# A hybrid encoder trunk on one core: buffers, engines and instruction order at the end of the recurrent scan and at the start of two output projections

## The chip, the core and the metric

The kernel runs on one core of a Trainium2 chip. Its engines work side by side, each through its own list of instructions in a fixed order: TensorE (PE in the profile) multiplies matrices, VectorE (DVE), ScalarE (ACT) and GpSimd (POOL) work on tiles, and SyncE (SP) issues most transfers between device memory and SBUF. An instruction waits until its operands are there and its output tile is free, and whatever stands behind it on the same engine waits with it. The metric is the device time of one execution in microseconds, the median of several runs.

## The reference

Two batches (256 prompt tokens, 1024 sample tokens, 1024 channels) go through two layers. Layer 0 mixes tokens with a bidirectional recurrence, layer 1 with neighbourhood attention. Each ends in an output projection, a residual sum and a squared-ReLU MLP. What matters here:

```
y = sum over both directions of _wkv_scan(...)            # per head, 64 wide
mu = mean(y); var = mean((y - mu)^2)                      # per token and head
y = (y - mu) * rsqrt(var + GN_EPS) * lnx_g + lnx_b
y = y + bonus * v
g = sigmoid(xg @ g1) @ g2                                 # the gate, 160 inner channels
x = x + (y * g) @ w_o                                     # layer 0
x = x + sq_relu_mlp(rms_norm(x, g_mlp), w_up, w_down)
...
x = x + attention(...) @ w_no                             # layer 1 (na_o in the reference)
x = x + sq_relu_mlp(rms_norm(x, g_mlp), w_up, w_down)
```

## The kernel before

Matrices are multiplied in three passes. An operand is split into a high part (a cast to fp32r, on ACT, tile names with h or hi) and a low part (operand minus high part, names with l or lo), and `mm3` sums high·high, high·low and low·high. Tokens come in three segments `SEGS`: segment 0 is the prompt (256 columns), 1 and 2 are the two halves of the sample (512 each). A tile `x13` is channel block 3 of segment 1. In the trace buffer numbers are left out; `x` stands for all of them.

**Scan.** Ten jobs of 16 steps run one after the other. Work is put in by due times (`at(t, f)`). In each step ACT copies the state `S` (L1101), the vectors `up`, `uv` and the output `y` or `y2` from PSUM, and DVE multiplies `zz` (L1008). After a job, `scan_post` normalises its output in two halves: mean, square, variance, scaling (DVE and ACT), the factor `lnx_g` (L1162) and the sum with the bonus (L1198), four transposes on PE into `zps`, a copy to the tile `zt` (L1207, ACT) and eight stores of `zt` to the scratch array `z_d` (L1212). For the last job (`left == 0`) the stores go through SP, sixteen in all. Before, there is one `zt` buffer.

**Gate.** `gate_begin` puts work into the last job: loads of the gate's operands into `graw`, their seven casts (L1331, L1334), the first two weights of `w_o` with their two casts (L1344), and the subtractions for the low parts on POOL. `gated` then makes 24 units (8 channel blocks times 3 segments): a load of `z_d` into `ot` (L1369, six buffers), four matrix products on PE, one multiply-add on DVE (L1374), a cast on ACT (L1376), a subtraction on DVE or POOL (L1377).

**mixer7**, called once for `w_o` and once for `w_no`. Its first stretch is the loop `for m in range(8)`: for output block m of segment 1, `dense` makes 24 products of 128x512, `take` adds the residual (L1410, DVE) and stores the sum (L1472, SP), `square` adds its square to `ms1` (ACT, POOL). Inside the loop weights are loaded three ahead into four ring slots and cut into high and low part (L1500 on ACT, L1407 on DVE). The weights are used twice. The second use, in the order `order = [0, 4, 1, 5, ...]`, serves segments 0 and 2. Its first three weights (here called order0, order1, order2) are loaded and cut inside the loop, at m = 5, 6 and 7. The fourth, order3, and the scaling of the finished `x1k` tiles (`ahs`, `als`, L1523, L1525; and L1528 in place) belong to the events behind the loop. Weight number n (0 to 7 the first use, 8 onwards the second) lies in ring slot n mod 4, so order0 takes the slot of weight 4 and order3 takes that of weight 7.

The order on an engine is set by a scheduler that moves instructions, except inside a `manual_schedule`, which keeps the engines that it names in the order of the program. Instructions from outside can still be placed among those of such a block. Before, `gated` had none, and the first stretch named SP alone.

Of the kernel before, what the change touches and what calls it, by code (L numbers as in the profile page):

```python
# [5 lines left out]
F32 = mybir.dt.float32  # L6
F32R = mybir.dt.float32r
AF = mybir.ActivationFunctionType
ALU = mybir.AluOpType
# [4 lines left out]
P = 128  # L14
# [47 lines left out]
class Trunk:  # L62
# [766 lines left out]
    def at(self, t, f):  # L829
        self.todo.append((t, len(self.todo), f))  # L830
# [304 lines left out]
    def scan_post(self, at, J, grp, left):  # L1135

        nc = self.nc
        for half in range(2):
            st = {}
# [12 lines left out]
                bonus = self.bonus.rearrange("p m c -> p (m c)")[:, o0:2 * o1 - o0].rearrange("p (x c) -> p x c", x=2)[:, :, 0:4]  # L1152
                nc.vector.tensor_tensor(out=st["bv"].rearrange("p (x c) v -> p x c v", x=2), in0=view(J["v"]), in1=each(bonus), op=ALU.mult)

            end = nc.gpsimd if left or half == 0 else nc.vector

            def lnx(st=st, runs=runs, y=y, end=end):
                t = y()
# [44 lines left out]
                    nc.tensor.transpose(ps[:, b].rearrange("p e t -> p (e t)"), y()[:, b // 2, b % 2 * 2:b % 2 * 2 + 2].rearrange("p c v -> p (c v)"), self.ident)  # L1203

            def p5(st=st, runs=runs):
                zt = self.yp.tile([P, 4, 2, 64], F32, name="zt", tag="zt", bufs=1)
                nc.scalar.copy(zt, st["zps"])  # L1207
                for x, (m, c0) in enumerate(runs):
                    dst = self.scr["z_d"][m].rearrange("(e v) (c t) -> e v c t", e=2, t=64)
                    for par in range(2):  # L1210
                        for e in range(2):
                            (nc.gpsimd if left else nc.sync).dma_start(dst[e, :, c0 + par:c0 + 4:2], zt[64 * par:64 * par + 64, 2 * x:2 * x + 2, 1 - e])  # L1212
# [87 lines left out]
    def gate_begin(self):  # L1300


        nc, tc = self.nc, self.tc
        at = lambda t, f, *x: self.at(16.0 * (len(self.jobs) - 1) + t, lambda: f(*x))

        def begin():
            self.ectx.close()
            self.m7ctx, self.gctx = ExitStack(), ExitStack()
            pool = lambda c, name, bufs: c.enter_context(tc.tile_pool(name=name, bufs=bufs, reuse_waits="tile", side="right"))
            self.mixer_weights(self.m7ctx, False)  # L1310
            gp = self.gp = pool(self.gctx, "gp", 1)
            self.gate = [[gp.tile([P if i < 2 else 96, n], F32R, name=nm + "hls"[i]) for i in range(3)] for nm, n in (("sg", T), ("g", 1024))]
            gp.tile([P, 512], F32, name="graw", tag="graw", bufs=7)
            self.wo = []

        def load(src, c0, c1, stacked):
            raw = self.gp.tile([P, 512], F32, name="graw", tag="graw", bufs=7)
            raw = raw[:, :c1 - c0]
            if stacked:
                for j in range(3):  # L1320
                    nc.sync.dma_start(raw[32 * j:32 * j + 32], src[P:P + 32, c0:c1])
            else:
                nc.sync.dma_start(raw, src[:P, c0:c1])
            self.graws.append(raw)

        def cut(i, c0, c1, stacked):
            raw = self.graws.pop(0)
            hi, lo, st = (z[:, c0:c1] for z in self.gate[i])
            if stacked:
                low = slice(32, 64) if i else slice(64, 96)  # L1330
                nc.scalar.copy(st, raw[:96])  # L1331
                nc.gpsimd.tensor_tensor(out=st[low], in0=raw[low], in1=st[low].bitcast(F32), op=ALU.subtract)
            else:
                nc.scalar.copy(hi, raw)  # L1334
                nc.gpsimd.tensor_tensor(out=lo, in0=raw, in1=hi.bitcast(F32), op=ALU.subtract)

        def wload(m):
            nc.sync.dma_start(self.m7["raw"][:, m], self.a["w_o"][m])

        def weight(m):  # L1340
            M = self.m7
            raw, (hi, lo) = M["raw"][:, m], M["ring"][m]
            M["turn"][0] += 1
            nc.scalar.copy(hi, raw)  # L1344
            nc.gpsimd.tensor_tensor(out=lo, in0=raw, in1=hi.bitcast(F32), op=ALU.subtract)
            self.wo.append((hi, lo))
        self.graws = []
        at(2.0, begin)
        parts = [(i, c0, min(c0 + 512, n), st) for i, n in ((0, T), (1, 1024)) for st in (0, 1) for c0 in range(0, n, 512)]
        for k, (i, c0, c1, st) in enumerate(parts):  # L1350
            src = self.a["g2"] if i else self.scr["sg2_d"]
            t = 7.0 + 0.9 * k
            at(t - 2.0, load, src, c0, c1, st)
            at(t, cut, i, c0, c1, st)
        for m in range(2):
            at(8.5 + m, wload, m)
            at(11.55 + 1.8 * m, weight, m)

    def gated(self, bank, src):

        nc, act = self.nc, self.act
        with self.gctx, self.tc.tile_pool(name="go", bufs=1, reuse_waits="tile", side="right") as gp:
            (sh, sl, ss), (gh, gl, gs) = self.gate
            todo = [(0, k) for k in range(KT)] + [(s, k) for s in (1, 2) for k in range(KT - 1)] + [(1, KT - 1), (2, KT - 1)]
            for s, k in todo:
                c0, c1 = SEGS[s]
                n = c1 - c0
                t = gp.tile([P, 512], F32, name="ot", tag="ot", bufs=6)[:, :n]
                nc.sync.dma_start(t, self.scr[src][k, :, c0:c1])  # L1369
                ks = slice(k * P, (k + 1) * P)  # L1370
                ps = bank()
                self.mm3(ps[:, :n], gh[:, ks], gl[:, ks], sh[:, c0:c1], sl[:, c0:c1], True, False)
                nc.tensor.matmul(ps[:, :n], gs[:, ks], ss[:, c0:c1], start=False, stop=True)
                nc.vector.scalar_tensor_tensor(out=t, in0=t, scalar=self.v(V_LNB, k), in1=ps[:, :n], op0=ALU.add, op1=ALU.mult)  # L1374
                hi, lo = (z[:, c0:c1] for z in act[k])
                nc.scalar.copy(hi, t)  # L1376
                (nc.gpsimd if k % 2 else nc.vector).tensor_tensor(out=lo, in0=t, in1=hi.bitcast(F32), op=ALU.subtract)  # L1377

    def mixer_weights(self, ctx, both):

# [10 lines left out]
    def mixer7(self, layer, x_src, wname, dst, src=None, gnext=None):  # L1391

        nc, tc, a, act = self.nc, self.tc, self.a, self.act
# [27 lines left out]
        with ExitStack() as ctx:  # L1421
# [70 lines left out]
            order = [0, 4, 1, 5, 2, 6, 3, 7]  # L1492
            todo = [*range(len(wo), 8), *order]

            with tc.manual_schedule(engines={mybir.EngineType.SP}):
                for m in range(8):
                    w = wo.pop(0)
                    while len(wo) < 3:
                        raw, (hi, lo) = wraw(todo.pop(0)), slot()
                        nc.scalar.copy(hi, raw)  # L1500
                        sub(V, lo, raw, hi.bitcast(F32))
                        wo.append((hi, lo))
                    if m == 0:
                        xload(1, 0, 4)
                    elif m < 3:
                        xload(1, 2 * m + 2, 2 * m + 4, m - 1)
                    elif m < 7:
                        xload(2, 2 * m - 6, 2 * m - 4, m - 1)
                    else:
                        xload(0, 0, 8, m - 1)  # L1510
                    take(1, m, dense(w, 1))
                    f = square(1, m)
                    if f:
                        f()
# [49 lines left out]
            for i, m in enumerate(order):  # L1564
                t = MS * i
# [1249 lines left out]
```

## Time and profile before

| what | value |
|---|---|
| median of 3 runs | 3889.02 us (3874.99, 3889.02, 4441.08) |
| profiled execution, its time | 3891.0 us |
| its span | 3889.2 us |
| busy PE, DVE, ACT, POOL | 93%, 71%, 47%, 52% of the span |
| last job's end and gate | about 1290 to 1372 us of the span |
| first stretch with w_o, with w_no | 1369 to 1410 us, 2951 to 2995 us |

The time of the execution is 1.8 us more than its span. Positions below are microseconds from the start of the span. "Idle before" in a row is the time that the engine did nothing ahead of this instruction, and the arrow names what ended it.

### The profile page before, as it was taken

To read this page: it belongs to the slowest core of one execution; us is meant where nothing else is said; L and a number is where in the kernel's file an instruction comes from. 1 tells how busy PE (TensorE), PEld (TensorE's weight loads), DVE (VectorE), ACT (ScalarE), POOL (GpSimd) and SP (SyncE) were. 2 spreads that over 40 slices of the span, in tenths; PEclk is the share of its full clock that TensorE was granted. 3 is DMA by queue.
4 is the path that set the end of the run, shared out by engine and by line. 5 is a ranking of instruction groups with operands and counts; after the bars stand their busy time and mean duration, and the time that the engine had idled before them with its cause. 6 is when DMAs were issued, how large, how long until landed. Compare 5 with 4: busy or idle time off the path is not lost.

```text
span 3889.2 us, 82949 instructions
## 1 busy us (share of the span) xinstructions
PE 3611.9 (93%) x32308; PEld 2979.9 (77%) x32308; DVE 2746.5 (71%) x4265; ACT 1809.9 (47%) x4065; POOL 2017.6 (52%) x2037
## 2 busy tenths in 40 slices
PE   6889998887878799999999999999999999999999
PEld 4766668766766587888888889777777788888888
DVE  7897976477776457777577771466676777767777
ACT  6776763344545445555421132456565455542111
POOL 5451111356566535444588870355454544448887
PEclk8998989889999899999999999999999999999999
DMA  3326666667687453555566635333345255556664
GB/s 110 90 85 212 233 229 186 156 149 176 151 177 169 121 181 120 204 216 212 190 232 234 233 116 162 99 81 74 85 101 185 82 216 212 210 202 219 232 226 162
DMA packets 489847, 654.09 MB, mean 168 GB/s; under 512 B 172752, under 2 KB 347056, under 8 KB 489456
## 3 DMA queue, kind: packets, MB, share of 16 engines
q1 hardware_dynamic: 398416, 436.30, 37.4%
q0 software_dynamic: 44336, 151.15, 11.8%
q10 hardware_dynamic: 46704, 61.35, 4.6%
q8 instruction: 255, 4.18, 0.5%
q14 instruction: 136, 1.11, 0.1%
HBM read 405.47 MB, written 254.41 MB: 170 GB/s over the span
## 4 chain that ended last, share of the span: by engine, by line
PE 44%; DVE 15%; DMA 8%; ACT 6%; issue 5%; POOL 5%; SPq 1%; DVEq 0%; POOLq 0%; ACTq 0%
PE pd L1404 19%; PE ps L1404 8%; DMA h_d<-ho 5%; PE kps L1003 2%; DVE ho L1407 2%; PE ps L108 2%; DVE wlo L1407 2%; POOL tT L1407 1%; PE ps L109 1%; PE ps L110 1%; ACT ho L1705 1%; PE bo L1044 1%; PE ba L1044 1%; PE op L2724 1%; DVE q L894 1%
## 5 line engine op out<-in xcount | busy, mean ns | idle before, releaser
L1404 PE MATMUL pd<-h,whi 128*128 128x512 f32 (+1 forms) x2656 | 697.0, 352 | 0.0
L1410 DVE TENSOR_TENSOR acc<-acc,pd 128x1024 f32<-128x1024 f32 x464 | 559.1, 1207 | 179.8 <-PE pd L1404 146.2
L1404 PEld LDWEIGHTS pd<-h,whi 128*128 128x128 f32 x2656 | 468.2, 189 | 67.9
L1404 PE MATMUL pd<-h,wlo 128*128 128x512 f32 (+1 forms) x1328 | 465.7, 351 | 0.0
L1404 PE MATMUL ps<-ahs,whi 128*128 128x512 f32 x768 | 303.8, 396 | 9.1 <-ACT tq L1748 5.8
L1404 PE MATMUL ps<-als,whi 128*128 128x512 f32 x768 | 300.0, 391 | 2.2 <-DVE als L1525 1.5
L1404 PE MATMUL ps<-ahs,wlo 128*128 128x512 f32 x768 | 299.1, 389 | 0.0
L1404 PEld LDWEIGHTS pd<-h,wlo 128*128 128x128 f32 x1328 | 250.9, 189 | 34.1
L1008 DVE TENSOR_TENSOR zz<-kps,cst 128x512 f32<-128x512 f32 x160 | 110.7, 692 | 179.7 <-ACT ll L1013 179.5
L1864 ACT CAST whi<-rsum 128x512 fp32r<-128x512 f32 x112 | 69.7, 623 | 297.5 <-POOL rsum L1407 162.6
L2638 POOL TENSOR_TENSOR s<-s,mx 128x384 f32<-128x384 f32 (+1 forms) x154 | 119.8, 788 | 156.9 <-DVE mx L2635 146.3
L1864 ACT CAST whi<-raw 128x512 fp32r<-128x512 f32 x128 | 79.3, 620 | 259.9 <-PE pd L1404 256.5
L1003 PE MATMUL kps<-x 64*64 64x128 f32 (+1 forms) x2560 | 169.6, 320 | 23.6 <-issue 17.9
L1407 POOL TENSOR_TENSOR wlo<-raw,whi 128x512 fp32r<-128x512 f32 (+1 forms) x122 | 161.4, 1323 | 56.3 <-ACT whi L1864 55.7
L1404 PE MATMUL ps<-ahp,whi 128*128 128x256 f32 x640 | 179.5, 280 | 0.0
L1404 PE MATMUL ps<-alp,whi 128*128 128x256 f32 x640 | 178.5, 279 | 0.0
L1404 PE MATMUL ps<-ahp,wlo 128*128 128x256 f32 x640 | 178.4, 279 | 0.0
L1404 PEld LDWEIGHTS ps<-ahs,whi 128*128 128x128 f32 x768 | 144.3, 188 | 43.9 <-ACT tq L1748 11.3
L1404 PE MATMUL ps<-op,whi 128*128 128x512 f32 x512 | 165.9, 402 | 11.6 <-DVE op L1407 6.0
L1407 POOL TENSOR_TENSOR wlo<-rsum,whi 128x512 fp32r<-128x512 f32 (+1 forms) x114 | 150.2, 1317 | 42.2 <-ACT whi L1864 38.4
L1404 PEld LDWEIGHTS ps<-als,whi 128*128 128x128 f32 x768 | 144.3, 188 | 33.4 <-DVE als L1525 3.2
L1410 POOL TENSOR_TENSOR rsum<-raw 128x512 f32<-128x512 f32 x60 | 77.4, 1290 | 177.8 <-DMA raw<-in_w_up_dram 165.5
(462 smaller groups left out, 11208.2 us busy)
## 6 DMA issues: line engine op xcount, KB each, us to landing
h<-h_d POOLq DMA_DIRECT2D x116, 1024.0 KB, 8.1
h_d<-ho SPq DMA_DIRECT2D x204, 512.0 KB
x<-x_d SPq DMA_DIRECT2D x80, 512.0 KB
raw<-in_w_up_dram SPq DMA_DIRECT2D x64, 512.0 KB
raw<-in_w_down_dram SPq DMA_DIRECT2D x32, 1024.0 KB
x_d<-ar ACTq DMA_DIRECT2D x32, 512.0 KB
x_d<-bk ACTq DMA_DIRECT2D x32, 512.0 KB
h_d<-ho SPq DMA_DIRECT2D x60, 256.0 KB
```

The lines of the kernel that those rows point to most:

```text
L108: mm(ps, sh, mh, start=first, stop=False)
L109: mm(ps, sh, ml, start=False, stop=False)
L110: mm(ps, sl, mh, start=False, stop=last)
L894: nc.vector.tensor_tensor(out=q[:, 0:jj, jj:], in0=q[:, 0:jj, jj:], in1=tv, op=ALU.add)
L1003: mm(J["kp"][out, e, 192 * c + 192 - w:192 * c + 192], x[es, b, 2 * pr + c], x[es, 5 - w // 64:5, 2 * pr + c], start=True, stop=True)
L1008: nc.vector.tensor_tensor(out=z, in0=src[:, :, :, :P], in1=self.mask[d].unsqueeze(1).unsqueeze(1).to_broadcast([P, 2, 2, P]), op=ALU.mult)
L1044: mm = lambda out, a, b, start, stop: nc.tensor.matmul(out, a, b, start=start, stop=stop, skip_group_check=True)
L1404: mul(ps, w[wi], b[bi], start=first and i == 0, stop=last and i == 2, skip_group_check=True)
L1407: eng.tensor_tensor(out=out, in0=x, in1=y, op=ALU.subtract)
L1410: eng.tensor_tensor(out=out, in0=x, in1=y, op=ALU.add)
L1864: nc.scalar.copy(hi, src)
L2638: nc.gpsimd.tensor_tensor(out=s()[:, :nk], in0=s()[:, :nk], in1=K["mx"][:, 2:3].to_broadcast([P, nk]), op=ALU.mult)
```

## The change

There are five edits. `zt` gets two buffers. The last job's first half does L1162 and L1198 on DVE, as its second half did before. The nine casts of `gate_begin` go from ACT to DVE, with due times a little moved. `gated` keeps program order on PE, DVE, ACT and POOL, and issues each subtraction one unit later. The first stretch of `mixer7` keeps program order on PE, DVE, ACT and POOL as well as on SP.

```
-            end = nc.gpsimd if left or half == 0 else nc.vector
+            end = nc.gpsimd if left else nc.vector
...
-                zt = self.yp.tile([P, 4, 2, 64], F32, name="zt", tag="zt", bufs=1)
+                zt = self.yp.tile([P, 4, 2, 64], F32, name="zt", tag="zt", bufs=2)
...
-                nc.scalar.copy(st, raw[:96])
+                nc.vector.tensor_copy(out=st, in_=raw[:96])
...
-                nc.scalar.copy(hi, raw)
+                nc.vector.tensor_copy(out=hi, in_=raw)
...
-            nc.scalar.copy(hi, raw)
+            nc.vector.tensor_copy(out=hi, in_=raw)
...
-            t = 7.0 + 0.9 * k
+            t = 6.78 + 0.9 * k
...
-            at(11.55 + 1.8 * m, weight, m)
+            at(11.7 + 2.0 * m, weight, m)
...
-        with self.gctx, self.tc.tile_pool(name="go", bufs=1, reuse_waits="tile", side="right") as gp:
+        E = mybir.EngineType
+        back = [lambda: None]
+        with self.gctx, self.tc.tile_pool(name="go", bufs=1, reuse_waits="tile", side="right") as gp, self.tc.manual_schedule(engines={E.PE, E.DVE, E.Activation, E.Pool}):
...
-                (nc.gpsimd if k % 2 else nc.vector).tensor_tensor(out=lo, in0=t, in1=hi.bitcast(F32), op=ALU.subtract)
+                back.append(lambda eng=nc.gpsimd if k % 2 else nc.vector, lo=lo, t=t, hi=hi: eng.tensor_tensor(out=lo, in0=t, in1=hi.bitcast(F32), op=ALU.subtract))
+                back.pop(0)()
+            back.pop(0)()
...
-            with tc.manual_schedule(engines={mybir.EngineType.SP}):
+            with tc.manual_schedule(engines={mybir.EngineType.PE, mybir.EngineType.DVE, mybir.EngineType.Activation, mybir.EngineType.Pool, mybir.EngineType.SP}):
```

Behind the gate's edits the lines of the changed kernel are two to four higher (L1410 becomes L1414, L1500 becomes L1504, L1523 becomes L1527, L1542 becomes L1546).

Three places show how the instructions move. The first is SP at the end of the scan. Before, six of the eight prompt loads of `ot` stand some forty rows ahead of the stores of `zt`, and the rest behind them.

```order
L1369 DMA ot<-z_d 128x256 x4
...
L1369 DMA ot<-z_d 128x256 x2
...
L1489 DMA raw<-in_w_o_dram 128x1024 x2
L1212 DMA z_d<-zt 64x2x64 x16
L1369 DMA ot<-z_d 128x256 x2
L1369 DMA ot<-z_d 128x512 x16
L1459 DMA x_19778<-in_xT_dram 128x512
```

In the changed kernel SP has this order there.

```order
L1321 DMA graw<-in_g_dram 32x512 x6
L1493 DMA raw<-in_w_o_dram 128x1024 x2
L1212 DMA z_d<-zt 64x2x64 x16
L1371 DMA ot<-z_d 128x256 x8
L1371 DMA ot<-z_d 128x512 x16
L1463 DMA x_19781<-in_xT_dram 128x512
```

All eight prompt loads have moved behind the sixteen stores. The second `zt` buffer also reaches 608 bytes per partition into the place where the first `ot` tile lies, which before began above all tiles of the scan.

The second place is ACT in the first stretch with `w_o`, from the square of `x13` on. Before, `x_19778` to `x_19785` are `x10` to `x17`; the casts from `rsum` are those of order0 and order1, the next two from `raw` those of order2 (L1500) and order3 (L1542).

```order
L1483 ACTIVATE tq<-x_19782 128x512
L1500 CAST whi<-rsum 128x1024
L1483 ACTIVATE tp<-x_19783 128x512
L1500 CAST whi<-rsum 128x1024
L1523 ACTIVATE ahs_19489<-x_19778,vec 128x512
L1483 ACTIVATE tq<-x_19784 128x512
L1500 CAST whi<-raw 128x1024
L1542 CAST whi<-raw 128x1024
L1483 ACTIVATE tp<-x_19785 128x512
L1528 ACTIVATE x_19778<-x_19778,vec 128x512
L1523 ACTIVATE ahs_19497<-x_19782,vec 128x512
```

In the changed kernel `x_19781` to `x_19788` are `x10` to `x17`, and ACT has this order.

```order
L1527 ACTIVATE ahs_19489<-x_19781,vec 128x512
L1487 ACTIVATE tq<-x_19785 128x512
L1546 CAST whi<-raw 128x1024
L1532 ACTIVATE x_19781<-x_19781,vec 128x512
L1527 ACTIVATE ahs_19497<-x_19785,vec 128x512
L1504 CAST whi<-rsum 128x1024
L1487 ACTIVATE tp<-x_19786 128x512
L1504 CAST whi<-rsum 128x1024
L1487 ACTIVATE tq<-x_19787 128x512
L1504 CAST whi<-raw 128x1024
L1487 ACTIVATE tp<-x_19788 128x512
```

The cast of order3 has moved from behind those of order0, order1 and order2 to a place ahead of all three, and two scalings have moved with it.

The third place is DVE in the same stretch, from the residual sum of `x14` on. Before:

```order
L1410 TENSOR_TENSOR x_19782<-ps,x_19782 128x512
L1407 TENSOR_TENSOR wlo<-raw,whi 128x1024
...
L1410 TENSOR_TENSOR x_19783<-ps,x_19783 128x512
L1407 TENSOR_TENSOR wlo<-rsum,whi 128x1024
...
L1410 TENSOR_TENSOR x_19784<-ps,x_19784 128x512
L1407 TENSOR_TENSOR wlo<-rsum,whi 128x1024
...
L1525 SCALAR_TENSOR_TENSOR als_19490<-x_19778,vec,ahs_19489 128x512
L1410 TENSOR_TENSOR x_19785<-ps,x_19785 128x512
L1407 TENSOR_TENSOR wlo<-raw,whi 128x1024 x2
```

In the changed kernel:

```order
L1414 TENSOR_TENSOR x_19785<-ps,x_19785 128x512
L1529 SCALAR_TENSOR_TENSOR als_19490<-x_19781,vec,ahs_19489 128x512
L1411 TENSOR_TENSOR wlo<-raw,whi 128x1024
L1411 TENSOR_TENSOR wlo<-rsum,whi 128x1024
...
L1414 TENSOR_TENSOR x_19786<-ps,x_19786 128x512
L1411 TENSOR_TENSOR wlo<-rsum,whi 128x1024
...
L1414 TENSOR_TENSOR x_19787<-ps,x_19787 128x512
L1411 TENSOR_TENSOR wlo<-raw,whi 128x1024
...
L1414 TENSOR_TENSOR x_19788<-ps,x_19788 128x512
```

`als0` and the low part of order3 (from `raw`) now stand ahead of the low part of order0 (from `rsum`), and the sums of `x15`, `x16` and `x17` stand behind the low parts of order0, order1 and order2 in turn. The stretch with `w_no` changes in the same way on both engines.

## Rows read from the trace of the kernel before

**Rows 1.** Busy time by stretch: length, then each engine, granted clock, DMA share, GB/s.

```profile
1290.00:1320.00 30.00, 22.59 (x649) 18.60 (x651) 8.16 (x12) 18.29 (x56) 22.88 (x26) 0.97 0.27 75
1368.00:1372.00 4.00, 0.97 (x4) 0.47 (x4) 3.50 (x5) 2.37 (x4) 2.77 (x3) 1.00 0.89 277
1400.00:1440.00 40.00, 40.00 (x223) 34.64 (x222) 24.04 (x38) 23.50 (x35) 11.16 (x8) 1.00 0.48 166
1480.00:1520.00 40.00, 30.89 (x128) 21.68 (x128) 32.61 (x40) 20.00 (x35) 19.08 (x12) 0.87 0.17 60
2990.00:3020.00 30.00, 30.00 (x167) 25.91 (x166) 20.08 (x32) 19.07 (x29) 7.20 (x5) 1.00 0.46 152
```

**Rows 2.** Timeline of ACT, end of the scan: start, duration, instruction, idle before.

```profile
1312.72 0.27 ACT L1101 COPY S<-bo 128x128 f32<-128x128 f32 x1
...
1318.03 1.04 ACT L1500 CAST whi<-raw 128x1024 fp32r<-128x1024 f32 x1 [2.45 <-DMA raw<-in_w_o_dram]
1318.98 0.26 ACT L1101 COPY S<-bo 128x128 f32<-128x128 f32 x1
...
1323.21 1.03 ACT L1500 CAST whi<-raw 128x1024 fp32r<-128x1024 f32 x1
...
1326.52 0.27 ACT L1108 COPY y<-bo 128x128 f32<-128x128 f32 x1 [0.85 <-PE bo L1044]
...
1333.88 0.58 ACT L1207 COPY zt<-zps 128x512 f32<-128x512 f32 x1
1341.85 0.58 ACT L1207 COPY zt<-zps 128x512 f32<-128x512 f32 x1 [7.38 <-DMA z_d<-zt]
```

**Rows 3.** Timeline of DVE from the last job's first half to the gate.

```profile
1325.42 1.23 DVE L1190 TENSOR_TENSOR rqt<-rqr 128x8 f32<-128x8 f32 x1
...
1329.70 0.69 DVE L1166 TENSOR_REDUCE mu<-y 128x8 f32<-128x512 f32 x1 [1.78 <-POOL y L1112]
...
1335.86 0.69 DVE L1198 TENSOR_TENSOR y<-y,bv 128x512 f32<-128x512 f32 x1
1343.75 0.48 DVE L1374 SCALAR_TENSOR_TENSOR ot<-ot,vec,ps 128x256 f32<-128x256 f32 x1 [7.19 <-PE ps L1373]
...
1350.25 0.48 DVE L1374 SCALAR_TENSOR_TENSOR ot<-ot,vec,ps 128x256 f32<-128x256 f32 x1 [1.63 <-DMA ot<-z_d]
...
1352.00 1.50 DVE L1374 SCALAR_TENSOR_TENSOR ot<-ot,vec,ps 128x512 f32<-128x512 f32 x2 [0.26 <-DMA ot<-z_d]
```

**Rows 4.** Timeline of SP (the queue's own instructions), same stretch.

```profile
1334.49 13.08 SPq L1212 DMA_DIRECT2D z_d<-zt  x16
1348.13 11.88 SPq L1369 DMA_DIRECT2D ot<-z_d  x13
```

**Rows 5.** Groups by line and shape, DVE copies: busy us, mean ns, idle before.

```profile
L2368 DVE COPY re<-rs 128x512 f32<-128x512 f32 x16 | 13.4, 836 | 0.0
```

**Rows 6.** Timeline of ACT, first stretch with w_o and behind it.

```profile
1405.70 1.05 ACT L1500 CAST whi<-rsum 128x1024 fp32r<-128x1024 f32 x1 [3.83 <-DMA rsum<-in_w_o_dram]
1406.65 0.72 ACT L1523 ACTIVATE ahs<-x,vec 128x512 fp32r<-128x512 f32 x1
...
1411.84 1.05 ACT L1542 CAST whi<-raw 128x1024 fp32r<-128x1024 f32 x1
...
1413.32 0.71 ACT L1528 ACTIVATE x<-x,vec 128x512 f32<-128x512 f32 x1
```

**Rows 7.** Timeline of DVE, same stretch.

```profile
1406.78 1.23 DVE L1407 TENSOR_TENSOR wlo<-rsum,whi 128x1024 fp32r<-128x1024 f32 x1 [1.47 <-ACT whi L1500]
...
1410.06 0.69 DVE L1410 TENSOR_TENSOR x<-ps,x 128x512 f32<-128x512 f32 x1 [0.18 <-PE ps L1404]
```

**Rows 8.** Instructions of line L1632, the norm's products: duration min/median/max, first and last start.

```profile
L1632 PE MATMUL ps<-ms,th x12: 378/590/1061, 1426.4 to 3074.9; 128*128 128x512 f32 x8, 128*128 128x256 f32 x4
```

**Rows 9.** Timeline of SP, first stretch with w_o: the load of order1.

```profile
1400.28 0.42 SPq L1489 DMA_DIRECT2D rsum<-in_w_o_dram  x1
```

**Rows 10.** Part 5 of the page: a sum of 128x512 on POOL: busy us, mean ns, idle before.

```profile
L1410 POOL TENSOR_TENSOR rsum<-raw 128x512 f32<-128x512 f32 x60 | 77.4, 1290 | 177.8 <-DMA raw<-in_w_up_dram 165.5
```

## The prediction

> **What bounds the kernel now.** PE is busy for most of the span (the table of the times), so time is won or lost where PE stands still. I read the table by stretch first, around the two places of the change [rows 1]. Between 1368 and 1372 PE works 0.97 of 4 us: the gate's last tiles are late. From 1400 to 1440, where the first use of `w_o` passes into the second, PE works 40.00 of 40 us, and from 2990 to 3020, the same place with `w_no`, 30.00 of 30. So a microsecond of waiting put in there has nothing to hide behind. At the scan's end the timelines show what each engine waits for: ACT's second `zt` copy waited 7.38 us for the stores of the first [rows 2], DVE stood for 7.19 us until PE gave it the gate's first product [rows 3], and SP issued sixteen `z_d` stores from 1334.49 to 1347.57 before the remaining `ot` loads [rows 4].
>
> **Scan and gate, step by step.** *Casts on DVE.* No row has such a cast of 128x512 on DVE; the nearest are a copy of that size at 0.84 us [rows 5] and a pass over the same size at 0.69 (`mu`) [rows 3]. I take 0.84 for seven and twice that for the two wide ones, 9.2 us in all. DVE works 8.16 of 30 us there [rows 1], so its idle time covers them; were the cover gone, 9.2 would be the loss. What ACT wins: one `w_o` cast (1318.03) stood 2.45 us for its load with the state copy `S` of 1318.98 behind it, 6.26 us after the `S` before (1312.72) [rows 2]. The changed order puts that cast one step later, so up to 2.45 us come free. Little of it stays, because the second such cast (1323.21) needs a load that can start only once the first is cut, and `uv` and the last `y2` (1326.52) stand behind it on ACT. I take 1.0 us.
>
> *lnx and the bonus sum of half 0 on DVE.* POOL's two passes leave the path ahead of the `y` sum for which `mu` waited 1.78 [rows 3]. In their place DVE has two passes of 0.69, the price of half 1's own (1335.86) [rows 3], and one low part of 1.23 [rows 7] ahead of the same `mu`. Gain 1.78, loss at most 2.6, of which the low part stood on DVE before too: zero.
>
> There is a rule against the casts' new place. The row shows a DVE operation on 128x8 elements that took 1.23 us [rows 3] at a time when POOL was subtracting. By the Trainium skill (GPSIMD Engine Reference, Key points) GpSimd shares its SBUF interfaces with VectorE and contends with VectorE instructions that have two SBUF inputs or run in a two-port mode. The trace agrees in that one row. By it the casts would hold up POOL, by an estimate of no more than their own 9.2 us, of which POOL's idle 7.1 of 30 us takes all but 2.1 [rows 1]: 3909 for the sum. The row is one of a short operation, and shows no cast, so I leave it out.
>
> *Two `zt` buffers.* Half 1 was summed at 1335.86 + 0.69 [rows 3]; with under 1 us for four transposes it was ready for its copy at some 1337.4, and waited until 1341.85 [rows 2]. With the 1.0 us above the second copy comes at 1336.4, 5.4 us earlier. But the changed order on SP takes most of this back. Before, six prompt tiles of `ot` lay in SBUF long before the gate, and DVE could multiply as soon as PE delivered (1343.75). Now all eight prompt loads stand behind the sixteen stores, and the first `ot` tile shares bytes with the second `zt`, so it also waits for the stores to have read it. Sixteen stores took 13.08 us with one stop between the halves; the eight behind the second copy's end (1341.85 + 0.58) took until 1347.57, or 0.64 each, which makes some 10.3 without the stop [rows 2, 4]. Starting 1 us earlier, at 1333.5, they end at 1343.8. A prompt load landed 2.1 us after its issue (1348.13 to the multiply-add that it released at 1350.25) [rows 4, 3]; I take the same for a store. So the first multiply-add comes at 1348.0, 4.3 us late. The first 128x512 unit needs a buffer that the third tile leaves behind its cast and subtraction, near 1350.5 by estimate, then a load of some 3 us, and comes at 1353.5 against 1352.00 [rows 3]. From there loads set the pace as before. Term: **+1.5 us**, between −5.4 (the loads turn out not to wait) and +4.3 (the whole delay of the first unit stays). The later subtraction and the order in `gated` I cost at nothing: they only exchange neighbours on DVE, while units wait for `ot`.
>
> **First stretch, step by step.** Let D be the end of the eighth product, the start of the sum of `x17` (1410.06) [rows 7]. Before, order0 was cut by then and PE went on without a stop. In the changed order ACT has the cast of order3 ahead of order0's. It writes the ring slot of weight 7, which PE reads until D. So ACT stands, and everything behind it.
>
> After D, on ACT: order3's cast 1.05, scaling in place 0.71, `ahs4` 0.72, order0's cast 1.05 [rows 6]. Starts follow about 0.1 before the shown ends (1405.70 + 1.05 against 1406.65), so this is 3.2 us. Then DVE cuts the low part, 1.23 [rows 7], less 0.23 that PE can spend on the first two products, which need only the high part (2 × 256 of the 24 × 768 columns that take 8.2 us, below), and PE starts in earnest some 4.3 us after D. *First stop: 4.3 us.* It is covered by nothing, since PE was busy throughout [rows 1].
>
> On DVE the sum of `x15` stands behind this low part and now ends at D + 5.4. Its store and then order1's load follow on SP, at D + 5.8. Order1 took 5.4 us from the issue of its load to its cast [rows 9, 6], so it lands at D + 11.2, and is cut (1.05 and 1.23) at D + 13.4. PE needs one output pair per (1426.4 − 1410.06) / 2 = 8.2 us [rows 8, 7], hence order1 at D + 12.5. *Second stop: 0.6.* In the same way the sum of `x16` stands behind that low part, order2's load behind it at D + 14.7, order2 is cut at D + 22.1, and the sum of `x17` comes at D + 22.7. PE's next item after order1's pair, at D + 21.4, is the norm's product, which needs `ms1` with the square of `x17`: 0.6 on ACT, as the `zt` copy of that size [rows 2], and 1.3 on POOL [rows 10], so D + 24.9. *Third stop: 3.5.* Together **8.4 us**, once with `w_o` and once with `w_no`, where the same rows stand in the same order. Between 4.3 (loads land sooner, the later two stops vanish) and 12.8. The upper end adds the clock: PE ran at a granted 0.87 over 1480 to 1520, a stretch with several waits, which is at most 5 us of 40; but it kept 1.00 after standing 3 of 4 us at 1368 to 1372 [rows 1], so I take none.
>
> Sum: 1.5 + 8.4 + 8.4 = **+18.3 us** on the profiled run's 3891.0, which lies 2.0 above the median of the runs. Forecast: 3889 + 18.3, about **3907 us**.
>
> **Rivals.** (a) *Only the first stops.* Loads land sooner than order1's did, so that order1 and order2 are cut in time, and `x17` is squared before the norm. The order of loads behind sums speaks against it; the margins of 0.6 and 0.7 us speak for it in part. 3889 + 1.5 + 2 × 4.3 = 3899.
>
> (b) *Faster: the scan's end decides.* If the `ot` loads don't wait for the last stores, the gate starts as soon as the second `zt` is copied: 5.4 us earlier. Of these 4.4 are the wait itself; with the 2.45 us of the blocked step, the 1.03 of the second cast ahead of the last `y2` and the 1.78 of `mu` all kept [rows 2, 3], the gate's end comes 9.7 us sooner. That alone decides for the other side from the point where it exceeds what the stops cost, 8.6 at least: 3889 − 9.7 + 8.6 = 3888, one microsecond faster. For it speaks the 7.38 us wait; against it that SP has the loads behind the stores.
>
> (c) *The order does less than it says.* The waits on the ring slot may end sooner than the last product of weight 7, or PE's late start may be swallowed by its later waits between 1480 and 1520 (9.1 of 40 us idle [rows 1]). Then only about 1.5 is left: 3891. Against it: those waits are for DVE and ACT work that shifts along with PE.
>
> (d) *More than forecast.* The clock falls in each first stop: 3889 + 4.3 + 2 × 12.8 = 3919.
>
> **How the numbers follow.** Forecast 0.50, (a) 0.17, (b) 0.10, (c) 0.13, (d) 0.10. The predicted time is the forecast's, 3907. The range must hold 8 in 10: from 3886, which leaves out most of (b) and the kernel's own spread downwards (two of its three runs lie at 3875 and 3889), to 3921. A measurement of this kernel can tell about 2% from no change, 78 us, and no case reaches that: within 2% 0.97, faster 0.01, slower 0.02.
>
> **What would show it.** In the profile of the changed kernel: PE idle by some 4 us right after the first stretch's last product, released by DVE's low part from `rsum`, with ACT's cast from `raw` of the events' line ahead of it, both with `w_o` and with `w_no`; another idle of 3 to 4 us before the norm's product, released by POOL's sum into `ms`; the second `zt` copy without its wait, and yet the gate's first multiply-add late and released by a load of `ot`. If PE passes without a stop from the first use of the weights to the second, the prediction is wrong in its main term; if the gate's last unit comes more than 5 us earlier relative to the last scan step, in the smaller one.

## The result, and the profile of the changed kernel

| | before | changed |
|---|---|---|
| median of 4 runs | 3890.05 us | 3921.46 us (3916.24 to 3927.70) |
| ratio, 95% interval | 1 | 1.0089 (1.0070 to 1.0108) |
| span of the profiled execution | 3889.2 us | 3915.7 us |

The change makes the kernel slower, by 0.9%: the ratio leaves out the run of before at 4441 us and means about 35 us, the medians differ by 31, the two profiled spans by 26.5. That is small, within 2%, but the interval of the ratio lies wholly above 1. I had forecast +18 us, 3907, with a range up to 3921.

Where did the time go? The first look is at stretches. These are stretches of rows 1 in the changed kernel, with the one from 1400 cut finer below it, and two short ones further on (length, busy time of each engine, granted clock, DMA share, GB/s).

```profile
1400.00:1440.00 40.00, 32.02 (x154) 26.96 (x153) 13.95 (x28) 14.30 (x21) 4.41 (x4) 0.87 0.51 169
1404.00:1408.00 4.00, 1.45 (x8) 1.25 (x9) 2.77 (x5) 1.93 (x4) 0.00 (x0) 0.94 0.00 1
1408.00:1412.00 4.00, 4.00 (x22) 3.87 (x22) 0.00 (x0) 0.44 (x1) 1.28 (x1) 0.63 0.93 294
...
1424.00:1428.00 4.00, 1.18 (x6) 0.63 (x4) 2.31 (x10) 1.37 (x2) 0.05 (x1) 1.00 0.20 49
1428.00:1432.00 4.00, 2.73 (x7) 1.70 (x8) 2.06 (x3) 1.64 (x3) 1.21 (x1) 0.50 0.89 282
1432.00:1436.00 4.00, 4.00 (x23) 3.96 (x23) 1.57 (x3) 2.93 (x5) 0.00 (x0) 0.64 0.13 46
...
1492.00:1496.00 4.00, 4.00 (x15) 3.53 (x15) 3.49 (x6) 1.66 (x3) 1.17 (x1) 0.50 0.17 66
...
2990.00:3020.00 30.00, 25.16 (x117) 20.60 (x116) 8.95 (x18) 7.93 (x11) 3.85 (x3) 0.94 0.48 167
3032.00:3036.00 4.00, 4.00 (x30) 3.74 (x30) 1.64 (x3) 2.36 (x6) 0.00 (x0) 1.00 0.46 155
```

Where PE worked 40.00 of 40 us before [rows 1], it works 32.02, and 25.16 where it worked 30.00 of 30 with `w_no`. Behind each stop with `w_o` the granted clock is down to about half for some microseconds: 0.63 from 1408, 0.50 from 1428, 0.64 from 1432.

The second look compares the same event in both traces. Each line gives its start before, its start after, and the difference.

| event | before | after | difference |
|---|---|---|---|
| last gate multiply-add (DVE) | 1370.28 | 1362.32 | −7.96 |
| a sum late in w_o's second use, which waits for PE in both | 1468.80 | 1474.39 | +5.59 |
| a sum in the MLP of layer 0 | 1607.39 | 1618.01 | +10.62 |
| first sum of w_no (`x10`) | 2956.73 | 2965.43 | +8.70 |
| a sum late in w_no's second use, which waits for PE in both | 3053.55 | 3073.27 | +19.72 |
| a sum in the MLP of layer 1 | 3140.96 | 3167.52 | +26.56 |
| last sum of the kernel | 3883.98 | 3910.44 | +26.46 |

So the place with `w_o` and the MLP's first weights cost 18.6 us (−7.96 to +10.62), and the place with `w_no` 17.9 (+8.70 to +26.56). Together that is 36 us, which agrees with the ratio. The two spans differ by less, because the changed kernel reached the first place 8.0 us early. The −7.96 at the gate's end is mostly older than the change's first effect: the fourteenth last copy of `S` in the scan starts at 1273.90 before and at 1267.77 after, 6.1 earlier. Two executions drift apart by some microseconds in stretches that the change doesn't touch (by 1.9 between the two places).

Now the waits. These are PE's stops in the timeline of the changed kernel, first stretch with `w_o` and behind it (start, duration, instruction, idle before and its releaser).

```profile
1397.37 0.50 PE L1408 MATMUL ps<-ahs,wlo 128*128 128x512 f32 x1 [0.26 <-DVE x L1462]
1405.79 0.38 PE L1408 MATMUL ps<-ahp,whi 128*128 128x256 f32 x1 [3.12 <-ACT whi L1504]
1407.05 0.39 PE L1408 MATMUL ps<-ahp,wlo 128*128 128x256 f32 x1 [0.76 <-DVE x L1462]
1429.27 2.07 PE L1636 MATMUL ps<-ms,th 128*128 128x512 f32 x2 [4.09 <-POOL ms L1414]
```

The stops that I had described are there: 3.88 us for order0 (3.12 for its high part, 0.76 for its low part, behind which the `x` copies run), 4.09 for the norm's product. With the first 0.26 they make 8.2 us. From −7.96 to +5.59 the loss is 13.55, so 5.3 us are not idle time. Most of them are the clock. In each of the four stretches below 1.00 from 1404 to 1436, the share of the clock that was not granted, times the time that PE worked, is what it lost: 0.06 × 1.45 + 0.37 × 4.00 + 0.50 × 2.73 + 0.36 × 4.00 = 4.4 us. The other 0.9 stay open.

With `w_no` PE's longest stops are these two, the first again with 0.76 us for the low part behind it.

```profile
3007.48 0.38 PE L1408 MATMUL ps<-ahp,whi 128*128 128x256 f32 x1 [3.12 <-ACT whi L1504]
...
3030.75 1.12 PE L1636 MATMUL ps<-ms,th 128*128 128x512 f32 x2 [3.29 <-POOL ms L1414]
```

With two short ones of 0.53 and 0.43 us they make 8.1 us, out of 11.0 lost there (+8.70 to +19.72).

But the rows of DVE, ACT and SP show another cause than the one that I had named. DVE in the changed kernel:

```profile
1364.04 0.69 DVE L1414 TENSOR_TENSOR x<-ps,x 128x512 f32<-128x512 f32 x1 [0.97 <-PE ps L1408]
1369.97 1.23 DVE L1411 TENSOR_TENSOR wlo<-rsum,whi 128x1024 fp32r<-128x1024 f32 x1 [5.25 <-ACT whi L1504]
...
1371.24 0.68 DVE L1414 TENSOR_TENSOR x<-ps,x 128x512 f32<-128x512 f32 x1
...
1388.52 0.68 DVE L1414 TENSOR_TENSOR x<-ps,x 128x512 f32<-128x512 f32 x1
1396.09 1.23 DVE L1411 TENSOR_TENSOR wlo<-raw,whi 128x1024 fp32r<-128x1024 f32 x1 [6.89 <-ACT whi L1504]
...
1397.35 0.68 DVE L1414 TENSOR_TENSOR x<-ps,x 128x512 f32<-128x512 f32 x1
...
1407.04 0.68 DVE L1414 TENSOR_TENSOR x<-ps,x 128x512 f32<-128x512 f32 x1
1415.57 1.23 DVE L1411 TENSOR_TENSOR wlo<-rsum,whi 128x1024 fp32r<-128x1024 f32 x1 [7.85 <-ACT whi L1504]
...
1416.83 0.68 DVE L1414 TENSOR_TENSOR x<-ps,x 128x512 f32<-128x512 f32 x1
...
1426.40 0.68 DVE L1414 TENSOR_TENSOR x<-ps,x 128x512 f32<-128x512 f32 x1
```

ACT:

```profile
1395.00 1.05 ACT L1504 CAST whi<-raw 128x1024 fp32r<-128x1024 f32 x1 [5.08 <-DMA raw<-in_w_o_dram]
...
1402.52 1.04 ACT L1546 CAST whi<-raw 128x1024 fp32r<-128x1024 f32 x1 [3.38 <-PE ps L1408]
...
1404.71 1.03 ACT L1504 CAST whi<-rsum 128x1024 fp32r<-128x1024 f32 x1
```

SP:

```profile
1389.63 0.38 SPq L1476 DMA_DIRECT2D xn_d<-x  x1
1390.07 7.60 SPq L1493 DMA_DIRECT2D raw<-in_w_o_dram  x2
...
1398.71 0.38 SPq L1476 DMA_DIRECT2D xn_d<-x  x1
1399.14 8.21 SPq L1493 DMA_DIRECT2D rsum<-in_w_o_dram  x2
```

Follow one round: the sum of `x13` starts at 1388.52, its store is issued at 1389.63, and weight 7's load right behind it at 1390.07. The cast follows when the load has landed (1395.00), the cut at 1396.09, and behind the cut on DVE the sum of `x14` at 1397.35. That sum has its store and the load of order0 behind it on SP, and so on. This is a ring: each round's first step waits for the last step of the round before. A round lasts 8.8 us, and later 9.6 to 9.8, where before the sums came every 5.44. The ring begins at the first sum (1364.04), behind which the second waits for a cut weight until 1371.24, and not behind the eighth product. PE does not stop at once, because weights are loaded three ahead. This lead shrinks by some 3 us in each round, and is used up where PE waits 0.26 us for the low part of weight 7 (1397.37). Over eight sums the lag grows: the sum of `x17` starts at 1426.40, 16.3 later than before (1410.06 [rows 7]), though the gate had ended 8.0 earlier. From the first sum to the eighth it took 62.36 us against 37.45.

The fourth loss comes from the same lag, and I had not seen it: the MLP's first weights. Before, their load was issued at 1456.62, now at 1467.25, since on SP it stands behind stores of sums that are still late. POOL waits for that load before it can sum the weights, ACT's cast waits for POOL, the prompt's scaling `ahp` stands behind that cast, and DVE's `alp` waits for `ahp`. Timelines of POOL, ACT and DVE of the changed kernel:

```profile
1473.21 1.29 POOL L1414 TENSOR_TENSOR rsum<-raw 128x512 f32<-128x512 f32 x1 [5.07 <-DMA raw<-in_w_up_dram]
```

```profile
1483.46 1.05 ACT L1681 CAST whi<-rsum 128x1024 fp32r<-128x1024 f32 x1 [4.81 <-POOL rsum L1411]
1484.42 0.91 ACT L1527 ACTIVATE ahp<-x,vec 128x256 fp32r<-128x256 f32 x2
```

```profile
1484.96 1.10 DVE L1529 SCALAR_TENSOR_TENSOR alp<-x,vec,ahp 128x256 fp32r<-128x256 f32 x2 [4.83 <-ACT ahp L1527]
```

The same cast and `alp` in the kernel before:

```profile
1472.20 1.05 ACT L1677 CAST whi<-rsum 128x1024 fp32r<-128x1024 f32 x1 [1.98 <-POOL rsum L1407]
```

```profile
1473.69 2.05 DVE L1525 SCALAR_TENSOR_TENSOR alp<-x,vec,ahp 128x256 fp32r<-128x256 f32 x2 [0.65 <-ACT ahp L1523]
```

They stood 11.3 us earlier, while PE is only 5.6 late there. PE now waits for `alp` three times, 3.6 us in all, and is 10.6 late behind it. The two longer waits:

```profile
1488.19 0.38 PE L1408 MATMUL ps<-alp,whi 128*128 128x256 f32 x1 [1.46 <-DVE alp L1529]
...
1491.09 0.58 PE L1408 MATMUL ps<-alp,whi 128*128 128x256 f32 x1 [1.89 <-DVE alp L1529]
```

Here too a part is the clock and not idle time: it is at 0.50 from 1492 to 1496, while PE works all of the 4 us.

### The profile page after: what moved, and what is told of

Its sections match the earlier page's. It is cut to its first block, busy times and chain, and to the rows that moved or that the text cites. A ratio compares the mean times of both kernels' runs of the same rounds, so it can differ in the third digit from the quotient of the medians.

```text
span 3915.7 us, 82906 instructions
## 1 busy us (share of the span) xinstructions
PE 3621.1 (92%) x32308; PEld 2986.5 (76%) x32308; DVE 2750.3 (70%) x4279; ACT 1806.0 (46%) x4053; POOL 2013.7 (51%) x2035
## 4 chain that ended last, share of the span: by engine, by line
PE 40%; DVE 16%; DMA 9%; ACT 7%; issue 6%; POOL 5%; SPq 1%; DVEq 0%; ACTq 0%; POOLq 0%
PE pd L1408 18%; DMA h_d<-ho 5%; PE ps L1408 4%; DVE ho L1411 2%; PE kps L1003 2%; DVE wlo L1411 2%; PE ps L108 2%; POOL tT L1411 1%; PE ps L109 1%; PE ps L110 1%; ACT ho L1709 1%; PE vps L527 1%; PE vps L528 1%; PE vps L529 1%; PE bo L1044 1%
## 5 line engine op out<-in xcount | busy, mean ns | idle before, releaser
L1414 DVE TENSOR_TENSOR acc<-acc,pd 128x1024 f32<-128x1024 f32 x464 | 559.1, 1207 | 179.7 <-PE pd L1408 145.9
L1408 PE MATMUL ps<-op,whi 128*128 128x512 f32 x512 | 166.1, 403 | 11.3 <-DVE op L1411 6.0
L1411 POOL TENSOR_TENSOR wlo<-rsum,whi 128x512 fp32r<-128x512 f32 (+1 forms) x114 | 150.2, 1317 | 42.5 <-ACT whi L1868 38.5
L1414 POOL TENSOR_TENSOR rsum<-raw 128x512 f32<-128x512 f32 x60 | 78.4, 1307 | 179.5 <-DMA raw<-in_w_up_dram 166.1
L1411 DVE TENSOR_TENSOR wlo<-raw,whi 128x1024 fp32r<-128x1024 f32 (+1 forms) x86 | 134.7, 1567 | 50.8 <-ACT whi L1504 41.6
```

Of the source, the lines that this page charges most:

```text
L1408: mul(ps, w[wi], b[bi], start=first and i == 0, stop=last and i == 2, skip_group_check=True)
L1411: eng.tensor_tensor(out=out, in0=x, in1=y, op=ALU.subtract)
L1414: eng.tensor_tensor(out=out, in0=x, in1=y, op=ALU.add)
```

## The experiments

"Sums" are the starts of the eight sums of the first stretch with `w_o` on DVE. Edits are against the changed kernel unless said. Ratios are to the kernel before, timed beside each of them on the same chip.

**One edit undone, and that edit alone.**

```
e1_sp_only:     with tc.manual_schedule(engines={SP}):                        # first stretch, as before
e2_order_only:  the kernel before, with engines={PE, DVE, ACT, POOL, SP} there
```

> The changed kernel with its fifth edit undone: the first stretch of mixer7 names SP alone again. Theory L (the loop's own pace): in program order DVE cuts the weight for m+3 ahead of the sum of block m, and that weight's load stands on SP behind the store of the sum before, so a round of the loop lasts load, cast, cut, sum, store (8.6 to 9.8 us in the changed kernel's trace) in place of 5.44; sums and second-use weights come late, PE stops three times and its clock falls. Theory C (the cast of order3 ahead of order0's on ACT) has another cause in the same edit. Both expect here: no stop of PE between 1400 and 1480 and none in the stretch with w_no, sums 5.44 us apart, 36 us less than the changed kernel, 3882 to 3892 us.

> The kernel before with the fifth edit alone. Both theories expect the whole loss here, 2 x 18 us: 3920 to 3930 us, with PE's stops after the first use of w_o and of w_no and before the norm's product. If the other four edits shared in the loss, it would be below 3910.

Measured: e1_sp_only 3883.37 us, ratio 1.0000 (0.9985 to 1.0015); e2_order_only 3918.22, ratio 1.0086 (1.0067 to 1.0105). The fifth edit holds the whole loss, and the other four together are worth nothing that the times can tell. In e1_sp_only PE works 40.00 of 40 us between 1400 and 1440, and its sums are 5.44 apart.

**The ring opened on SP.** Loads of weights are issued one round earlier, ahead of the sum and store of that round; program order stays on all five engines.

```
+                ahead = []
                 for m in range(8):
                     ...
-                        raw, (hi, lo) = wraw(todo.pop(0)), slot()
+                        raw, (hi, lo) = ahead.pop(0) if ahead else wraw(todo.pop(0)), slot()
                     ...
+                    if m < 7:
+                        ahead.append(wraw(todo.pop(0)))
```

> The changed kernel, program order kept, but each weight's load is issued one round of the loop earlier, so that it no longer stands behind the store of the sum of the round before. Theory L: the rounds no longer last a load's time, the sums come 5.4 to 6 us apart, order0 to order2 are cut in time, no stop of over 1 us, 3882 to 3895 us. If the order on DVE (cut ahead of sum) were enough for the loss, sums would stay late and the time above 3910.

Measured: 3884.98 us, ratio 1.0004 (0.9990 to 1.0019). The stretches of this kernel, as above:

```profile
1400.00:1440.00 40.00, 40.00 (x222) 34.66 (x221) 23.79 (x40) 22.02 (x34) 11.02 (x9) 1.00 0.43 147
...
2990.00:3020.00 30.00, 30.00 (x167) 25.92 (x166) 18.11 (x30) 19.48 (x32) 8.58 (x7) 1.00 0.41 136
```

DVE's first sum of the stretch and the eighth:

```profile
1369.53 0.69 DVE L1414 TENSOR_TENSOR x<-ps,x 128x512 f32<-128x512 f32 x1 [1.56 <-PE ps L1408]
...
1407.63 0.69 DVE L1414 TENSOR_TENSOR x<-ps,x 128x512 f32<-128x512 f32 x1 [0.50 <-PE ps L1408]
```

The first and the last of the eight lie 38.1 us apart, or 5.44 a round, and each waits for PE, not for a weight. So program order as such costs nothing that the times can tell: what costs is the place of the loads in it. In this kernel the scheduler also puts order3's cast behind order0's, so it doesn't yet tell the ring from my own cause.

**My cause by itself.** The events' cast and cut of order3 are put later, which moves them behind those of order0 to order2 on ACT and DVE.

```
-                    ev(t + 0.4, wo_cut, i + 3, 0)
-                    ev(t + 1.5, wo_cut, i + 3, 1)
e4:  +               ev(t + (9.0 if i == 0 else 0.4), wo_cut, i + 3, 0)      # 10.1 for part 1
e11: +               ev(t + (8.0 if i == 0 else 0.4), wo_cut, i + 3, 0)      # 8.3 for part 1
```

> The changed kernel, but the cast and the cut of order3 are put 8.6 us later among the events, which places them behind those of order0 to order2 on ACT and DVE. Theory C: ACT no longer waits for the end of the eighth product ahead of order0's cast, so the first stop of 3.9 us and what follows from it go: 3888 to 3902 us. Theory L: order0's load was issued only at 1399.14, behind the store of x14, and cannot be cut before some 1405.7 anyway; sums stay 8.6 to 9.8 us apart, all stops stay within 1 us, 3914 to 3926 us.

In e4_order3_late the cast of order3 falls behind that of the next weight, and the two trade their ring slots and their places in the second use. Products are of the same number and shape, but some take the wrong weight, so this kernel does not compute the reference's result, and only its time is of use. e11_order3_behind keeps the slots as they were.

> The changed kernel with order3's cast and cut 7.6 us later among the events, still ahead of those of the weight after it, so that ring slots stay as they are; it computes everything (e4_order3_late let order3 and the weight after it trade slots). On ACT order3's cast then stands behind those of order0 to order2. Theory C: 3888 to 3902 us, no first stop. Theory L: sums as late as in the changed kernel, first stop of 3 us or more, 3912 to 3926 us.

Measured: e4_order3_late 3918.91 us, ratio 1.0083 (1.0059 to 1.0106); e11_order3_behind 3922.55, ratio 1.0100 (1.0084 to 1.0117). Nothing is won. ACT's timeline in e11_order3_behind, order0's and order1's casts:

```profile
1402.68 1.04 ACT L1504 CAST whi<-rsum 128x1024 fp32r<-128x1024 f32 x1 [3.20 <-DMA rsum<-in_w_o_dram]
...
1412.34 1.05 ACT L1504 CAST whi<-rsum 128x1024 fp32r<-128x1024 f32 x1 [5.92 <-DMA rsum<-in_w_o_dram]
```

And PE's stops in the same kernel:

```profile
1403.78 0.38 PE L1408 MATMUL ps<-ahp,whi 128*128 128x256 f32 x1 [3.02 <-ACT whi L1504]
1405.04 0.38 PE L1408 MATMUL ps<-ahp,wlo 128*128 128x256 f32 x1 [0.76 <-DVE x L1462]
1427.13 2.07 PE L1636 MATMUL ps<-ms,th 128*128 128x512 f32 x2 [3.95 <-POOL ms L1414]
```

With nothing of order3 ahead of it, ACT stands all the same, now for the load of order0, and PE's stop is 3.02 + 0.76 us against 3.12 + 0.76. The cast of order3 only stood in a gap that was there anyway. My theory falls here.

**Which engine's program order.**

```
e9_dve_free:  engines={PE, ACT, POOL, SP}
e10_dve_sp:   engines={DVE, SP}
```

> The changed kernel, but the first stretch keeps program order on PE, ACT, POOL and SP and not on DVE. The scheduler then puts each cut of a weight one sum later on DVE, and order3's cast behind order0's on ACT. Theory L (the cut that waits for a load stands ahead of the next sum on DVE, and that load behind a store of a sum): the ring is open, sums 5.44 us apart, no stops: 3878 to 3890 us. If program order on ACT, POOL or SP were enough, 3910 or more.

> The changed kernel, with program order in the first stretch on DVE and SP alone. Theory L: the whole loss is here, sums 8.6 to 9.8 us apart and the same stops: 3914 to 3928 us. If ACT's program order is needed for it: 3895 or less.

Measured: e9_dve_free 3886.39 us, ratio 1.0013 (0.9997 to 1.0029), sums 5.44 apart (1375.98 to 1414.06), PE busy 40.00 of 40 us from 1400; e10_dve_sp 3924.63, ratio 1.0102 (1.0081 to 1.0122), sums 7.0 to 9.7 apart. Program order on DVE, beside that on SP, is enough for the loss, and without it there is none. Where DVE is free, the scheduler puts each cut one sum later, so a sum never waits for a load that was issued only behind the sum before. Breaking the ring at either link, on SP (e3_loads_early) or on DVE (e9_dve_free), ends it.

**The end of the scan.** With SP alone in the first stretch, one `zt` buffer again (e5), or five `ot` buffers (e6, where the `ot` tiles no longer reach into the second `zt`), or the nine casts back on ACT (e8); e7 has all five edits with early weight loads and five `ot` buffers.

```
e5_one_zt:  zt bufs=1      e6_ot5:  ot bufs=5      e7:  e3 with ot bufs=5
e8_casts_act:  nc.scalar.copy(hi, raw) in cut and weight, as before
```

> The changed kernel with SP alone in the first stretch (as e1_sp_only) and one zt buffer again. The first ot tile then shares no bytes with a zt tile, and six prompt loads go ahead of the stores. Theory P (the second zt buffer's gain is paid back by the lost early loads): the second zt copy again waits some 4 us for stores, the gate's first multiply-add follows PE and not a load, and from the last scan step to the end of the gate it takes as long as e1_sp_only within 2 us. If early loads were worth nothing (rival), it would be 4 to 5 us longer than e1_sp_only.

> The changed kernel with SP alone in the first stretch and five ot buffers in place of six, so that the ot tiles and the second zt tile share no bytes and five prompt loads go ahead of the stores. Theory P: DVE's first gate operation comes some 9 us earlier than in e1_sp_only, its first of 128x512 about 5 us, and the gate ends 4 us earlier measured from the last scan step: 3876 to 3884 us. Rival: the gate's end hangs on its sixteen 256 KB loads with one buffer fewer, and nothing is won: 3881 to 3890.

> The changed kernel with all five edits, the weights' loads issued one round earlier (as e3_loads_early) and five ot buffers. Both repairs together: no stop of PE behind the two first stretches and the gate's end 4 us earlier than in e3_loads_early; 3876 to 3886 us. If program order in the first stretch costs something beside the loads' place, it is above e6_ot5 by more than 5 us.

> The changed kernel with SP alone in the first stretch and the nine casts back on ACT. My term for the casts is a gain of 1.0 us at the last y2. If it holds, the stretch from 1280 to the last y2 is 1 to 2 us longer than in e1_sp_only, and the whole 1 us longer, too little for the times to show (3880 to 3890 us). If the casts are worth nothing, no difference; if they are worth the blocked step's 2.45 us and more, 3 us or above.

Measured: e5_one_zt 3880.37 us, ratio 0.9994 (0.9977 to 1.0011); e6_ot5 3877.61, 1.0001 (0.9985 to 1.0017); e7_loads_early_ot5 3882.88, 1.0009 (0.9996 to 1.0023); e8_casts_act 3887.32, 1.0013 (0.9997 to 1.0028). None can be told from the kernel before. The medians of e6 and e7 differ by 5.3 us, the ratios by 3, and their intervals overlap. So whether program order still costs a few microseconds once the loads are early isn't settled. DVE's first gate operation, its first of 128x512 and its last, in e6_ot5:

```profile
1322.42 0.48 DVE L1376 SCALAR_TENSOR_TENSOR ot<-ot,vec,ps 128x256 f32<-128x256 f32 x1 [3.17 <-PE ps L1375]
...
1333.45 0.75 DVE L1376 SCALAR_TENSOR_TENSOR ot<-ot,vec,ps 128x512 f32<-128x512 f32 x1 [0.20 <-DMA ot<-z_d]
...
1351.39 0.74 DVE L1376 SCALAR_TENSOR_TENSOR ot<-ot,vec,ps 128x512 f32<-128x512 f32 x1
```

Counted from the last `y2` on ACT (1309.20 in e6_ot5, 1314.74 in e1_sp_only), the first comes at 13.2 us against 22.0 in e1_sp_only (1336.76), so the early loads do bring the start forward by 8.8 us. The first unit of 128x512 comes at 24.3 against 27.5 (1342.26), and the last at 42.2 against 43.3 (1358.00). With one `zt` buffer and early loads (e5_one_zt) the last comes at 42.5. The gate's end moves by 1.1 us where I had expected 4, so the rival of e6 held. In e7 it comes 43.3 us behind `y2` against 45.6 in e3_loads_early, 2.3 earlier where I had expected 4. In e5 theory P held: the second copy waits again (8.02 us at 1334.70), and the gate still takes 0.7 less than in e1_sp_only. Differences of 1 to 3 us stay open here. Up to the gate the changed kernel and e1_sp_only have the same program, and yet the last gate operation lies 45.0 us behind `y2` in the one and 43.3 in the other. The worth of the casts is not settled either. From the fourteenth last copy of `S` to the last `y2` it takes 51.3 us with the casts on ACT (e8_casts_act) and 51.2 on DVE (e1_sp_only). But it takes 52.6 in the kernel before and 50.9 in e2_order_only, which run the same instructions up to there.

## Why the prediction was wrong

**Scan and gate, +1.5 us.** Not contradicted. The second `zt` copy lost its wait for the stores (it waits 3.35 us for the transposes at 1328.71), the first multiply-add came late and was released by a load of `ot` (1340.53, idle 13.09), as forecast. (The four transposes, put at under 1 us, took 1.09 before; nothing hangs on it.) Counted from the last `y2`, the gate's last multiply-add comes at 45.0 us against 43.8 before, 1.2 later. That is near my term, but less than the 1.7 by which the same program differs above, so it shows no more than that the term is small. Without the fifth edit the kernel equals the one before to 0.15% (e1_sp_only). Rival (b), that the scan's end pays more than the stops cost, is out.

**First stretch, 8.4 us each.** The direction was right, and the idle time came out near the forecast: first stop 3.9 (4.3), second none (0.6), third 4.1 (3.5), in all 8.2 us with a short one ahead. Two steps failed, and the cause that I gave for the first stop did too.

The first is a size that I set to zero. "It kept 1.00 after standing 3 of 4 us …, so I take none" about the clock: it fell to 0.50 to 0.64 for about 4 to 8 us behind the stops, which is 4.4 us with `w_o`. I had it as rival (d), at 3919, and with 0.10. (The 12.8 us per place there is less than what I named for it: 8.4 and at most 5 are 13.4.)

The second is where I let the delay begin and end. I began counting at D, with order3's cast on ACT, and ended with the norm's product. But the sums are late from the first round of the loop, because DVE has the cut of a weight ahead of the sum, and that weight's load stands behind the store of the sum before. I had used just these two links for order1 and order2 and not asked whether they close to a ring for the weights before them. As the lag is on DVE and SP and not on PE, it outlives the norm, delays the load of the MLP's first weights by 10.6 us, and costs another 5.0 us at the prompt's scaling (+5.59 to +10.62), and 6.8 with `w_no`. This term was missing.

With `w_o`: 8.2 idle, 5.3 more without idle time (4.4 of them the clock), and 5.0 at the MLP's first weights make 18.6. Two such places and nothing for the gate give 36 us, which the ratio (27 to 42 us) holds.

**The cause** that I named for the first stop, the ring slot of weight 7 under order3's cast, is refuted: with that cast put behind those of order0 to order2, the stop is still 3.8 us (e11_order3_behind). The waits that I described did take place in the changed kernel, but the load of order0, late in the ring, ends at nearly the same time. So that 3.9 came out near my 4.3 is luck. Rival (a), which left only the first stops, and (c), that later waits swallow them, are out as well: DVE and ACT came to that place 11.3 us late, with PE 5.6 late, and made it later still.

## What to carry to other kernels

Program order in a loop can close a ring across engines: cut ahead of sum on one queue, load behind store on another. Look in the order tables not only for what stands ahead of the late instruction, but for whether each round's first step waits for the last one's last; then the lag grows by (round through the ring − round through the bottleneck) in each round, 25 us here from the first sum to the eighth. What the bottleneck's lead doesn't cover of it falls due wherever the bottleneck next needs what is behind. When you price a stop of the matrix engine, look at the granted clock behind it too: here 8.2 us of idle time with `w_o` came with 4.4 us of clock, though one stop of 3.29 us with `w_no` came with none. And when one engine lags without the bottleneck stopping, follow its lag to the next stage that takes its work.

## What the hardware showed that I had not expected

With `w_o` TensorE's granted clock fell from 1.00 (2.4 GHz) towards 0.50 (1.2 GHz) behind two stops. The first (3.12 and 0.76 us) came after some 60 us of work with 0.26 us of idle time, the second (4.09 us) after 18 us of unbroken work. The clock was back at 1.00 some 4 to 8 us later (0.63 and 1.00 in the stretches from 1408 and 1412; 0.50, 0.64 and 1.00 from 1428, 1432 and 1436). It was at 0.50 from 1492 to 1496 too, behind the three waits for `alp` of 0.26, 1.46 and 1.89 us. Not every stop did this. With `w_no` the clock was 0.57 from 3008 to 3012, behind the first stop, but 1.00 from 3028 to 3036, at and behind the stop of 3.29 us that ended at 3030.75. In the kernel before it had stayed at 1.00 in the stretch with 3.0 us of idle time at 1368 to 1372 [rows 1].
